# A hybrid decoder step on one NeuronCore: the head is rebuilt around untouched inputs, the end of the key search is divided around a norm, and three rotary products change engine

## The chip, the cores and the metric

The kernel runs on one core of one Trainium2 chip. The metric is the time of one execution on the device in microseconds (us), as a median of several runs. The kernel before has a median of 1154.69 us over three runs, the lowest at 1154.56 and the highest at 1155.33 us.

## The reference

One layer of a decoder for a prompt of 1024 tokens and 8 sequences of 4 new tokens each (1056 columns in all), width 1024. What matters here, cut:

```
mod = silu(c) @ w_ada + b_ada                       # one row for the prompt, 8 for the samples
shift, scale, gate = split(mod, 3)
h = rms_norm(x, g_norm) * (1 + scale) + shift
qa,ka,va,za, qi,ki,wi, qr,kr,vr,zr, ga,gr = split(h @ w_in)
# indexer: for every query the 256 best keys, by sum over 4 heads of w * relu(qi . ki)
idx = top_k(where(key <= query, index_scores(qi, wi, ki), -inf), 256)
y_a = sparse_attend(qa, ka[idx], va[idx]) * silu(za)
# retention: 8 heads (4 pairs), chunks of 128 tokens with a running state per head
q_r, k_r = rotary(qr), rotary(kr) / 8
y_r = group_norm(retention(q_r, k_r, vr)) * g_ret * silu(zr)
x = x + gate * ((sigmoid(ga) * (y_a @ w_pa) + sigmoid(gr) * (y_r @ w_pr)) @ w_out)
return rms_norm(x) * g_final, and the new keys, values, indexer keys and states
```

A prompt query below position 256 has at most 256 admissible keys, so that nothing has to be searched for it.

## The kernel before

All values that are projected stand transposed, features on partitions and the 1056 tokens in columns. Each product of full precision is made of three matmuls: weights and inputs are split into a high part (a cast to the fp32r type) and a low part (the difference), and high x high, high x low and low x high are added up (`terms`, L210 to L212). The inputs' parts are the tiles `hh` and `hl`, one of each per 128 features, k = 0 to 7; a projection of 128 output features takes 8 x 3 matmuls for each of three chunks of 352 columns.

The program's parts that matter here, in their order:

- **The head.** SyncE's queue loads a table of constants (792 columns, the first 128 of them the identity), nine tiles of x (the samples' first), and the adaLN weights `w_ada` in 16 blocks of 512 KB. ScalarE squares each tile with a sum over its row (L286), VectorE makes the reciprocal roots (`rsqrt`), VectorE or GpSimd scales the tile by them (L293), TensorE transposes it (L296) and ScalarE and VectorE copy the two halves into `xr` (L298). For each k, `h_tile` multiplies two adaLN blocks by the conditioning (`ada_rows`, L204), selects the rows of the nine conditions (L309), applies scale and shift (L313, L316), and makes `hh` (ScalarE, L317) and `hl` (VectorE or GpSimd, L318). Behind each k, `start_two` has 18 matmuls of the first two projections (indexer keys, and indexer queries of heads 0 and 1), into six accumulators.
- **The weights of the later projections.** Each 512 KB block is loaded one projection ahead (`prefetch`, L190) and split (cast L196 on ScalarE; difference L197, by turns on VectorE and GpSimd).
- **The indexer.** The rest of its queries (`project(O_QI + 128, ...)`), the scores of blocks of 128 queries against the keys (L660, L661; blocks 2 to 7 only), and those of the samples.
- **The search.** For every query the 256th largest score is found bit by bit, 31 rounds, by counting the scores above a candidate. The counts of blocks 2 to 6 run on VectorE (L743), those of block 7 and the samples on ScalarE (L750). Then comes the end of the search: `exact` sharpens the two thresholds that ScalarE's counts have found (for the samples, then block 7), and `finish` writes a mask for each of the seven score tiles, the samples' first (j = 6), then block 7 (j = 5), then blocks 2 to 6.
- **Retention.** TensorE meanwhile works through the gates' projections and four pairs of heads, one after the other (`pair`, p = 0 to 3): keys and queries are projected and rotated (`rotated`, L459 to L461, with a copy that DMAs shift by half a head), the products of keys and values by chunk (L491) are summed up by one scan on VectorE (L493), ScalarE copies the states into `SD` (L495), and TensorE multiplies them by the queries (L514). The group norm of pair p ends with L582, kept as `normed[p]`.
- **The rest.** The attention with the found keys, the remaining projections, and the output, from about 526 us on.

What sets the order: every engine has one queue of instructions, filled at build time by a scheduler that interleaves the search with retention. `tc.issue_after(x)` puts the instructions made under it behind x in the scheduler's order, where they go to the same engine's queue. In the kernel before the whole end of the search stands under

```
with tc.issue_after(normed[2].ins):
    exact(1)
    exact(0)
    for j in range(NP - 1, -1, -1):
        finish(j)
```

so that VectorE meets it only behind the third pair's norm.

## Time and profile before

| profiled execution | |
|---|---|
| its own time | 1154.27 us |
| span of the trace | 1152.5 us |
| mean granted clock of TensorE | 0.989 |
| TensorE busy (weight loads beside it) | 1090.3 us, 95% (993.7) |
| VectorE busy | 674.0 us, 58% |
| ScalarE busy | 465.1 us, 40% |
| GpSimd busy | 335.0 us, 29% |
| moved by DMA | 182.56 MB, 158 GB/s in the mean |

TensorE's share says only how often it had something to do. Where it had not, a stretch of the span has to be looked at by itself, and which engine was busy in its place. The granted clock is the part of full speed at which the chip let TensorE run. In the rows, PE is TensorE's matmuls, PEld its weight loads, DVE VectorE, ACT ScalarE, POOL GpSimd, and SPq SyncE's queue of DMAs.

### The profile page before, as it was taken

How to read it: one execution, taken by the hardware profiler on the slowest of the kernel's cores; microseconds unless marked ns; L12 is line 12 of the kernel's file. 1: busy time of each engine (PE TensorE's matmuls, PEld its weight loads, DVE VectorE, ACT ScalarE, POOL GpSimd, SP SyncE). 2: the span in 40 equal slices, each digit the busy share in tenths (PEclk: the TensorE clock that was granted, in tenths of full speed). 3: DMA queues.
4: the chain of work that ended last, by engine and by line, in shares of the span. 5: the costliest groups of instructions: out<-in, count | busy, mean ns of one | idle time of the engine just before them, and what ended most of it. 6: DMA issues, size and time to landing. Idle time of an engine off the chain costs nothing. (4 is left out here: it accounts for less than half of the span.)

```text
span 1152.5 us, 20285 instructions
## 1 busy us (share of the span) xinstructions
PE 1090.3 (95%) x8016; PEld 993.7 (86%) x8016; DVE 674.0 (58%) x1585; ACT 465.1 (40%) x894; POOL 335.0 (29%) x259
## 2 busy tenths in 40 slices
PE   4999999999999999969999999999999999989997
PEld 3889989899989999968998999877988888888886
DVE  6856449999999536993132222201246777477745
ACT  5465445655655341123243332211336656333211
POOL 3413015023311611351331212143124434375000
PEclk9999999999999999988999999999999999999999
DMA  9913235134334424412686866597899931495321
GB/s 304 264 34 111 75 104 146 53 111 140 104 90 120 141 54 139 125 37 79 221 267 199 249 193 193 178 306 262 267 269 240 236 102 66 143 275 176 114 92 55
DMA packets 157956, 182.56 MB, mean 158 GB/s; under 512 B 18901, under 2 KB 129053, under 8 KB 156774
## 3 DMA queue, kind: packets, MB, share of 16 engines
q1 hardware_dynamic: 147928, 145.56, 42.9%
q0 software_dynamic: 9856, 35.66, 9.5%
q8 instruction: 63, 1.03, 0.4%
q14 instruction: 31, 0.25, 0.1%
q10 hardware_dynamic: 78, 0.06, 0.0%
HBM read 138.86 MB, written 38.60 MB: 154 GB/s over the span
## 5 line engine op out<-in xcount | busy, mean ns | idle before, releaser
L210 PE MATMUL pj<-hh,wh 128*128 128x352 f32 x1176 | 385.4, 328 | 6.0 <-ACT qrT L446 3.2
L211 PE MATMUL pj<-hl,wh 128*128 128x352 f32 x1176 | 381.2, 324 | 0.0
L212 PE MATMUL pj<-hh,wl 128*128 128x352 f32 x1176 | 381.0, 324 | 0.0
L210 PEld LDWEIGHTS pj<-hh,wh 128*128 128x128 f32 x1176 | 221.3, 188 | 13.2 <-issue 4.4
L211 PEld LDWEIGHTS pj<-hl,wh 128*128 128x128 f32 x1176 | 221.9, 189 | 5.7 <-issue 4.9
L212 PEld LDWEIGHTS pj<-hh,wl 128*128 128x128 f32 x1176 | 221.6, 188 | 3.9 <-issue 3.4
L743 DVE TENSOR_SCALAR_CACHE_REDUCE eq<-sc,cand 128x896 bf16<-128x896 f32 (+4 forms) x155 | 135.7, 875 | 2.3
L197 POOL TENSOR_TENSOR wl<-ws,wh 128x1024 fp32r<-128x1024 f32 (+1 forms) x33 | 63.1, 1913 | 174.8 <-ACT wh L196 156.4
L196 ACT CAST wh<-ws 128x1024 fp32r<-128x1024 f32 (+1 forms) x65 | 61.1, 940 | 108.5 <-PE pj L211 64.4
L197 DVE TENSOR_TENSOR wl<-ws,wh 128x1024 fp32r<-128x1024 f32 x32 | 41.4, 1294 | 62.2 <-ACT wh L196 61.3
L1084 POOL TENSOR_SCALAR lg<-lg,st 128x1024 f32<-128x1024 f32 (+7 forms) x64 | 47.4, 746 | 76.2 <-DVE st L1083 70.9
L750 ACT ACTIVATE ra<-sc,cand 128x1024 bf16<-128x1024 f32 x31 | 35.6, 1149 | 61.6 <-DVE cand L821 61.6
L930 POOL DMA_INDIRECT kv<-in_cache_k,idx x32 | 30.9, 966 | 98.8 <-PE str L960 80.8
L1082 ACT ACTIVATE lg<-lg,st 128x1024 f32<-128x1024 f32 (+7 forms) x64 | 49.5, 775 | 22.1 <-DVE st L1081 21.8
L962 DVE COPY kt<-str 128x512 f32<-128x512 f32 x32 | 22.1, 689 | 61.3 <-PE str L960 57.6
L589 ACT ACTIVATE raw<-pj 128x352 f32<-128x352 f32 x48 | 22.1, 461 | 74.7 <-PE pj L212 67.2
L930 POOL DMA_INDIRECT kv<-in_cache_v,idx x32 | 31.1, 973 | 71.2 <-PE sx L988 42.0
L1260 PE MATMUL pj<-wol,MH 128*128 128x512 f32 (+1 forms) x136 | 51.2, 377 | 0.0
L1259 PE MATMUL pj<-woh,MH 128*128 128x512 f32 (+1 forms) x136 | 51.2, 377 | 0.0
L1261 PE MATMUL pj<-woh,ML 128*128 128x512 f32 (+1 forms) x136 | 51.2, 377 | 0.0
L1097 PE MATMUL tr<-C,lg 128*128 128x128 f32 x288 | 43.7, 275 | 1.2 <-ACT pT L1099 0.5
L962 ACT COPY kt<-str 128x512 f32<-128x512 f32 x32 | 18.8, 589 | 55.1 <-PE str L960 44.1
(341 smaller groups left out, 2073.9 us busy)
## 6 DMA issues: line engine op xcount, KB each, us to landing
ws<-in_w_in SPq DMA_DIRECT2D x51, 512.0 KB
TG<-raw SPq DMA_DIRECT2D x16, 528.0 KB
rot<-in_rot SPq DMA_DIRECT2D x8, 1056.0 KB
wa<-in_w_ada SPq DMA_DIRECT2D x16, 512.0 KB
u<-TG SPq DMA_DIRECT2D x8, 528.0 KB
RT<-u SPq DMA_DIRECT2D x8, 528.0 KB
t<-TG SPq DMA_DIRECT2D x8, 528.0 KB
u<-RT SPq DMA_DIRECT2D x8, 528.0 KB
```

The costliest lines, as they stand in the source:

```text
L196: nc.scalar.copy(wh[:, :, :n], ws[:, :, :n])
L197: (nc.vector if len(order) % 3 else nc.gpsimd).tensor_sub(wl[:, :, :n], ws[:, :, :n], f32(wh[:, :, :n]))
L210: nc.tensor.matmul(p, wh[:, k], HH[k][:, sl], start=(k == 0), stop=False)
L211: nc.tensor.matmul(p, wh[:, k], HL[k][:, sl], start=False, stop=False)
L212: nc.tensor.matmul(p, wl[:, k], HH[k][:, sl], start=False, stop=(k == KT - 1))
L743: nc.vector.tensor_scalar(junk[:n, :W], sc, thr[:n, j:j + 1], 0.0, op0=op, op1=OP.add, accum_out=cnt[:n, j:j + 1])
L930: nc.gpsimd.indirect_dma_start(out=t.rearrange("p s c -> p (s c)"), out_offset=None, in_=cache.rearrange("g (r s) h d -> (g r) (s h d)", s ...
L1082: nc.scalar.activation(l, l, AF.Exp, bias=st[:, 2:3], scale=0.125, accum_out=st[:, 3:4])
L1084: nc.gpsimd.tensor_scalar(l, l, st[:, 0:1], 0.5, op0=OP.mult, op1=OP.mult)
L1259: nc.tensor.matmul(x, MH[:, k, tk], wh[:, k], start=(k == 0), stop=False)
L1260: nc.tensor.matmul(x, MH[:, k, tk], wl[:, k], start=False, stop=False)
L1261: nc.tensor.matmul(x, ML[:, k, tk], wh[:, k], start=False, stop=(k == KT - 1))
```

## The change

The x tiles are transposed as they land. Their squares are made beside that (those of tiles 1 and 4 on VectorE, by `SQD`), and the reciprocal norms are brought into a row that is the same on all partitions, `RB`, by matmuls of a matrix of ones with diagonal matrices (`norms`). `h_tile` multiplies the transposed tile by scale and norm in one instruction, ScalarE adds the shift while it makes `hh`, and VectorE the same while it makes `hl`, both in halves of 528 columns. GpSimd has no part in it. All adaLN blocks use the x tiles' buffers, eleven in all, and they are issued in one row; the weights of later projections are issued behind the last of them, and their split stands behind the last `hh` and `hl`. The constants are loaded in two parts. Queries of the indexer are projected for columns from 256 on only, in two chunks of 400 (`late`), in the first projections and in the second. Behind the search, `exact(1)`, `exact(0)` and the samples' mask are no longer ordered behind `normed[2]`, the other six masks are. The rotation of the third pair's queries and of the fourth pair's keys and queries is on VectorE.

The core of the diff:

```diff
-SQD = ()
+SQD = (1, 4)
...
+    late = [slice(256, 656), slice(656, TT)]
+
+    def start_two(W):
+        x, y = pl(), pl()
+        parts_ = [(p[:, :sl.stop - sl.start], sl, i) for p, sl, i in
+                  zip((pj(), pj(), x[:, :512], x[:, 512:], y[:, :512]), chunks + late, (0, 0, 0, 1, 1))]
         for k in range(KT):
-            for i, p in enumerate(banks):
-                terms(p, W[i // 3], k, chunks[i % 3])
-        return banks
+            for term in range(3):
+                for p, sl, i in parts_:
+                    nc.tensor.matmul(p, W[i][term == 2][:, k], (HL if term == 1 else HH)[k][:, sl],
+                                     start=(k == 0 and term == 0), stop=(k == KT - 1 and term == 2))
...
+        def x_block(i):
+            t = SEQ[i]
+            n, x = size(t), X[t]
+            p = pl().rearrange("p (k t) -> p k t", k=KT)
+            for k in range(KT):
+                nc.tensor.transpose(p[:, k, :n], x[:n, 128 * k:128 * k + 128], ident[:n, :n])
+            sq = BI[7]
+            if t in SQD:
+                nc.vector.tensor_tensor_reduce(out=sq[:n], in0=x[:n], in1=x[:n], scale=1.0, scalar=0.0,
+                                               op0=OP.mult, op1=OP.add, accum_out=ssq[:n, i:i + 1])
+            else:
+                nc.scalar.activation(sq[:n], x[:n], AF.Square, accum_out=ssq[:n, i:i + 1])
+            for g, copy in ((slice(0, 4), nc.scalar.copy), (slice(4, 8), nc.vector.tensor_copy)):
+                copy(XT[:, g, t * 128:t * 128 + n], p[:, g, :n])
+
+        def norms(i0, i1):
...
+            r = rsqrt(sp, v, i1 - i0)
+            p, c0 = pj(), 128 * SEQ[i1 - 4]
+            for i in range(i1 - 4, i1):
+                dg = sp.tile([128, 128], F32, name="dg", bufs=3)
+                nc.vector.tensor_scalar(dg, ident, r[:, i - i0:i - i0 + 1], None, op0=OP.mult)
+                o = 128 * (i - i1 + 4)
+                nc.tensor.matmul(p[:, o:o + 128], one, dg, start=True, stop=True)
+            nc.scalar.copy(RB[:, c0:c0 + 512], p)
...
+        def h_tile(k, pm):
+            shift = BB[:, k, 0:1]
+            nc.scalar.activation(AA[:, k], pm[:, 16:25], AF.Identity, bias=cg[:, k:k + 1], scale=cols[:, 24 + k:25 + k])
+            nc.scalar.activation(shift, pm[:, 0:1], AF.Identity, bias=cols[:, k:k + 1])
+            h = XT[:, k]
+            nc.vector.scalar_tensor_tensor(h[:, :T], h[:, :T], AA[:, k, 0:1], RB[:, :T], op0=OP.mult, op1=OP.mult)
...
+            for sl in (slice(0, 528), slice(528, TT)):
+                high = nc.scalar.activation(HH[k][:, sl], h[:, sl], AF.Identity, bias=shift)
+                rest = nc.vector.scalar_tensor_tensor(HL[k][:, sl], h[:, sl], shift, f32(HH[k][:, sl]), op0=OP.add, op1=OP.subtract)
+            return high, rest
...
+        for i in range(9):
+            x_block(i)
+            if i == 4:
+                norms(0, 5)
+        norms(5, 9)
...
     def prefetch():
         if order:
             f0 = order.pop(0)
-            split.append((f0, wsplit(wp, wload(wp, w_in, f0, 128), 128)))
+            with tc.issue_after(loads[-1].ins), tc.issue_after(head_ends[0].ins), tc.issue_after(head_ends[1].ins):
+                split.append((f0, wsplit(wp, wload(wp, w_in, f0, 128), 128)))
...
-            nc.gpsimd.tensor_tensor(x, x, RT_[:, :TT], op=OP.mult)
-            nc.gpsimd.tensor_tensor(y, y, RT_[:, TT:], op=OP.mult)
-            nc.gpsimd.tensor_tensor(x, x, y, op=OP.add)
+            e = nc.vector if p + a > 2 else nc.gpsimd
+            e.tensor_tensor(x, x, RT_[:, :TT], op=OP.mult)
+            e.tensor_tensor(y, y, RT_[:, TT:], op=OP.mult)
+            e.tensor_tensor(x, x, y, op=OP.add)
...
-            project(O_QI + 128, use_qi(2))
+            project(O_QI + 128, use_qi(2), late)
...
+            exact(1)
+            exact(0)
+            finish(NP - 1)
 
             with tc.issue_after(normed[2].ins):
-                exact(1)
-                exact(0)
-                for j in range(NP - 1, -1, -1):
+                for j in range(NP - 2, -1, -1):
                     finish(j)
```

The built order shows three places. First SyncE's queue in the head, from the first adaLN block on: `wa` before and `x` from `in_w_ada` now are the adaLN blocks, `ws` the weights of projections, `ptab` a page table. Before:

```order
L324 DMA wa<-in_w_ada 128x8x128 x3
L190 DMA ws<-in_w_in 128x8x128 x2
L324 DMA wa<-in_w_ada 128x8x128 x6
L190 DMA ws<-in_w_in 128x8x128
L324 DMA wa<-in_w_ada 128x8x128 x2
L190 DMA ws<-in_w_in 128x8x128
L324 DMA wa<-in_w_ada 128x8x128 x3
L190 DMA ws<-in_w_in 128x8x128
L324 DMA wa<-in_w_ada 128x8x128
L190 DMA ws<-in_w_in 128x8x128
L324 DMA wa<-in_w_ada 128x8x128
L673 DMA ptab<-in_page_table 16x8x1 x8
```

The same place of SyncE's queue now:

```order
L348 DMA x<-in_w_ada 128x8x128 x2
L189 DMA ws<-in_w_in 128x8x128 x2
L348 DMA x<-in_w_ada 128x8x128 x14
L189 DMA ws<-in_w_in 128x8x128 x2
L703 DMA ptab<-in_page_table 16x8x1 x8
```

Of the six blocks of projection weights, two still stand early (those of the first two projections); the four others stood between adaLN blocks, and now none does.

TensorE's queue at the end of the head, from the last adaLN products on (`pt<-x,scT`); `hh_82` and `hl_90` are the parts of tile 5, `hh_83` that of tile 6, and a `pj` or `pl` stands for an accumulator:

```order
L203 MATMUL pt<-x,scT 32x128 x16
L225 MATMUL pj<-hh_82,w 128x352 x2
L225 MATMUL pl<-hh_82,w 128x352
L225 MATMUL pl<-hh_82,w 128x400 x2
L225 MATMUL pj<-hl_90,w 128x352 x2
L225 MATMUL pl<-hl_90,w 128x352
L225 MATMUL pl<-hl_90,w 128x400 x2
L225 MATMUL pj<-hh_82,w 128x352 x2
L225 MATMUL pl<-hh_82,w 128x352
L225 MATMUL pl<-hh_82,w 128x400 x2
L321 MATMUL pt<-C,ar 128x16 x2
L225 MATMUL pj<-hh_83,w 128x352 x2
```

Behind the last adaLN products stand all 15 matmuls of tile 5, three of them 128x352 and two 128x400 for each of the three terms, then the selection for tile 7, then tile 6.

VectorE's queue at the end of the search. Before, from the last count (`eq,cnt`) on; `base` holds the thresholds, `wl` a low part of weights, `zsT` and `S` belong to the third pair:

```order
L743 TENSOR_SCALAR eq,cnt<-sc_772,cand 128x384
L757 TENSOR_SCALAR inc<-cnt 128x5
L819 TENSOR_TENSOR base<-base,inc 128x7
L197 TENSOR_TENSOR wl<-ws,wh 128x1024
L484 SCALAR_TENSOR_TENSOR zsT<-zt,zsT 128x352 x2
L493 SCALAR_TENSOR_TENSOR S<-dm,pt 128x512
```

The same place of VectorE's queue now, from the two exact thresholds on (L802 to L815; `scs` are the samples' scores):

```order
L802 TENSOR_SCALAR low<-base 128x1 x2
L803 SCALAR_TENSOR_TENSOR low<-base,low 128x1 x2
L804 TENSOR_TENSOR base<-base,low 128x1 x2
L773 TENSOR_SCALAR eq,cnt<-scs,base 32x1056
L196 TENSOR_TENSOR wl<-ws,wh 128x1024
L808 TENSOR_SCALAR eq<-scs,base 32x1056
L811 TENSOR_SCALAR flag<-cnt 128x1
L809 ISA ra,low<-eq,scs 32x1056
L809 ISA low 32x1
L491 TENSOR_TENSOR qrT<-qrT,rot 128x1056
L492 TENSOR_TENSOR tmp<-tmp,rot 128x1056
L812 TENSOR_TENSOR low<-low,flag 128x1
```

and a little further on in it, to the third pair's scan (`S<-dm,pt`):

```order
L516 SCALAR_TENSOR_TENSOR zsT<-zt,zsT 128x352
L826 SCALAR_TENSOR_TENSOR ra<-eq 32x1056
L827 SCALAR_TENSOR_TENSOR ra<-ra,rem,eq 32x1056
L828 SCALAR_TENSOR_TENSOR ra<-scs,base,ra 32x1056
L516 SCALAR_TENSOR_TENSOR zsT<-zt,zsT 128x352
L829 TENSOR_SCALAR bis<-ra 32x1056
L525 SCALAR_TENSOR_TENSOR S<-dm,pt 128x512
```

Between the search's last round and the third pair's scan VectorE now has the exact thresholds, the rotation of that pair's queries (L491 to L493) and the samples' mask (L825 to L829), where it had one split and two small products. From the end of the fourth pair on all five engines' queues are what they were.

## Rows read from the trace of the kernel before

**Rows 1.** The span cut into stretches, with the busy time of each engine in us and its instructions (x), TensorE's granted clock (PEclk), the mean busy share of the DMA engines and what they moved in GB/s.

```profile
0.00:14.00 14.00, 0.07 (x1) 0.07 (x2) 3.79 (x19) 8.39 (x14) 0.20 (x4) 1.00 0.87 309
14.00:37.20 23.20, 18.20 (x222) 14.90 (x222) 22.29 (x56) 11.35 (x23) 14.19 (x9) 1.00 1.10 286
37.20:69.10 31.90, 30.88 (x293) 28.71 (x294) 19.26 (x34) 12.15 (x18) 10.20 (x4) 1.00 0.69 175
...
155.00:388.00 233.00, 223.81 (x1577) 214.61 (x1576) 213.12 (x549) 133.42 (x234) 67.19 (x33) 1.00 0.39 115
388.00:447.40 59.40, 59.40 (x467) 56.67 (x467) 20.04 (x33) 18.24 (x33) 17.59 (x9) 0.99 0.36 103
447.40:509.60 62.20, 62.16 (x436) 61.22 (x435) 61.57 (x81) 14.21 (x27) 28.44 (x11) 1.00 0.36 104
509.60:520.90 11.30, 0.00 (x0) 0.00 (x0) 11.20 (x16) 3.04 (x4) 0.00 (x0) 0.62 0.17 47
520.90:526.00 5.10, 5.09 (x32) 4.86 (x34) 0.35 (x1) 0.00 (x0) 0.00 (x0) 0.50 0.05 10
...
sum 1152.50, PE 1090.33 PEld 993.72 DVE 674.00 ACT 465.13 POOL 335.01; mean PE 99.12 PEld 90.34 DVE 61.27 ACT 42.28 POOL 30.46
```

The columns of engines are PE, PEld, DVE, ACT and POOL, in this order.

**Rows 2.** TensorE's waits by line and by what released them: us in total, how many, the longest.

```profile
PE pl L514 <- ACT SD L495: 12.6, 2, 11.4
```

**Rows 3.** The timeline of SyncE's queue in the head: start, duration, and the DMAs that it issued.

```profile
32.70 1.63 SPq L190 DMA_DIRECT2D ws<-in_w_in  x1
...
48.54 1.63 SPq L190 DMA_DIRECT2D ws<-in_w_in  x1
```

**Rows 4.** TensorE's timeline: start, duration, line, and in brackets the idle time ahead with what ended it.

```profile
26.21 1.09 PE L296 MATMUL pl<-C,x 128*128 128x128 f32 x8
...
56.21 0.51 PE L309 MATMUL pt<-C,ar 128*128 128x16 f32 x4
...
58.16 0.65 PE L204 MATMUL pt<-wa,scT 128*32 128x128 f32 x16 [0.86 <-DMA wa<-in_w_ada]
...
59.80 0.32 PE L210 MATMUL pj<-hh,x 128*128 128x352 f32 x1
...
62.20 0.32 PE L210 MATMUL pl<-hh,x 128*128 128x352 f32 x1
...
90.33 0.40 PE L661 MATMUL pl<-kil,qs 128*128 128x512 f32 x1
...
91.72 0.39 PE L661 MATMUL pl<-kil,qs 128*128 128x512 f32 x1
```

**Rows 5.** What single instructions cost: the groups on the tiles x, xr and hl in the head (ns least, median and most, with first and last start), and one row each of VectorE's and GpSimd's timelines.

```profile
L286 ACT ACTIVATE sq<-x x9: 1038/1055/1062, 5.2 to 17.4; 128x1024 bf16<-128x1024 f32 x8, 32x1024 bf16<-32x1024 f32 x1
...
L298 ACT COPY xr<-pl x9: 265/585/587, 17.3 to 33.1; 128x512 f32<-128x512 f32 x8, 128x128 f32<-128x128 f32 x1
L298 DVE COPY xr<-pl x9: 282/679/692, 18.5 to 34.5; 128x512 f32<-128x512 f32 x8, 128x128 f32<-128x128 f32 x1
...
L318 DVE TENSOR_TENSOR hl<-xr,hh x5: 1248/1257/2357, 37.7 to 65.4; 128x1056 fp32r<-128x1056 f32 x5
...
122.28 0.88 DVE L667 SCALAR_TENSOR_TENSOR sc<-rl,wsc,sc 128x640 f32<-128x640 f32 x1 [1.24 <-ACT rl L663]
...
40.79 2.87 POOL L197 TENSOR_TENSOR wl<-ws,wh 128x1024 fp32r<-128x1024 f32 x1 [6.50 <-ACT wh L196]
```

**Rows 6.** VectorE's timeline from the search's last instruction to the fourth pair's scan.

```profile
387.56 0.17 DVE L819 TENSOR_TENSOR base<-base,inc 128x7 int32<-128x7 int32 x1
...
410.02 1.22 DVE L493 TENSOR_TENSOR_SCAN S<-dm,pt 128x512 f32<-128x512 f32 x1 [4.97 <-PE pt L491]
...
447.28 0.25 DVE L582 SCALAR_TENSOR_TENSOR tmp<-pt,gT,zsT 128x32 f32<-128x32 f32 x1 [1.57 <-PE pt L579]
...
465.58 0.69 DVE L799 TENSOR_SCALAR bis<-ra 32x1056 bf16<-32x1056 f32 x1
...
475.53 2.65 DVE L797 SCALAR_TENSOR_TENSOR ra<-ra,rem,eq 128x384 f32<-128x384 f32 x1
478.22 2.72 DVE L798 SCALAR_TENSOR_TENSOR ra<-sc,base,ra 128x384 f32<-128x384 f32 x1
...
481.53 1.95 DVE L799 TENSOR_SCALAR bi<-ra 128x384 bf16<-128x384 f32 x1
...
491.13 2.91 DVE L797 SCALAR_TENSOR_TENSOR ra<-ra,rem,eq 128x640 f32<-128x640 f32 x1
494.07 2.97 DVE L798 SCALAR_TENSOR_TENSOR ra<-sc,base,ra 128x640 f32<-128x640 f32 x1
...
517.35 1.22 DVE L493 TENSOR_TENSOR_SCAN S<-dm,pt 128x512 f32<-128x512 f32 x1
```

**Rows 7.** GpSimd's timeline in the same stretch: the first instruction of each of three rotations (the third pair's queries, the fourth pair's keys and queries).

```profile
390.94 2.48 POOL L459 TENSOR_TENSOR qrT<-qrT,rot 128x1056 f32<-128x1056 f32 x1 [9.48 <-DMA tmp<-qrT]
...
474.60 3.16 POOL L459 TENSOR_TENSOR krT<-krT,rot 128x1056 f32<-128x1056 f32 x1 [15.77 <-DMA tmp<-krT]
...
489.61 3.75 POOL L459 TENSOR_TENSOR qrT<-qrT,rot 128x1056 f32<-128x1056 f32 x1 [6.35 <-DMA tmp<-qrT]
```

**Rows 8.** The fourth pair's products of keys and values on TensorE's timeline, and the copies of its states on ScalarE's.

```profile
503.68 1.15 PE L491 MATMUL pt<-vtok,kd 128*64 128x64 f32 x32
...
518.60 2.26 ACT L495 COPY SD<-S 64x512 f32<-64x512 f32 x2 [3.85 <-DVE S L493]
```

More of the change, by code (lines that the diff above doesn't have):

```diff
@@ L183, in _hybrid_step @@
     gT = cst.tile([128, 4], F32, name="gT")
+    BI = {b: selp.tile([128, (b + 1) * 128], BF, name=f"bi{b}") for b in range(8)}
+    BIS = selp.tile([NS, LK], BF, name="bis")
     def wcols(src, k, f0, n):
@@ L315, in h_tile @@
[L315 to L324 removed]
+            return pm
@@ L590, in gates @@
             nc.sync.dma_start(TG[128 * j:128 * j + 128], t)
-    BI = {b: selp.tile([128, (b + 1) * 128], BF, name=f"bi{b}") for b in range(8)}
-    BIS = selp.tile([NS, LK], BF, name="bis")
     k_out, v_out, ki_out, st_out, ks_out, vs_out, kis_out, sts_out = outs[2:]
```

138 lines of the change are left out of this document (58 added, 80 removed).

## Prediction

> **What bounds the kernel now.** I read the stretches first [rows 1]: the span cut at the places where TensorE's state changes, with every engine's busy time. The reader is to see that TensorE is the engine with work nearly everywhere, 1090.3 of 1152.5 us, and where it is not: 14 us at the start, 5.0 of the next 23.2 us, 9.2 us in all of the search (155 to 388 us), and one hole of 11.3 us at 509.6 us in which VectorE is busy throughout. Next come TensorE's waits [rows 2]: the hole is one wait of 11.4 us for the copies of the fourth pair's states (SD, line 495). Then the head (everything up to the first projections' end at 69.1 us) in the SyncE queue's issues and in TensorE's timeline [rows 3, 4]: the last adaLN weights land when product L204 starts at 58.16 us, after a wait for the DMA. Then what single instructions cost [rows 5], and VectorE, GpSimd and the fourth pair's products around the hole [rows 6 to 8].
>
> Two facts decide. The head is a stream of loads: 286 to 309 GB/s from the start [rows 1]. And the hole is VectorE's: from 447.4 to 509.6 us it is busy for 61.6 of 62.2 us and in the hole for 11.2 of 11.3, while in the 59.4 us before that it had only 20.0 us of work [rows 1]. It may not start the end of the search before the third pair's norm (L582, 447.28 us), although the search itself ended at 387.7 us [rows 6].
>
> **Fewer columns for the indexer's queries.** Only queries from 256 on are searched, so columns 0 to 255 of both query projections go. Fifteen starts of the 352-column product lie 2.40 us apart, 0.160 us each; six of the 512-column product 1.39 us, 0.232 us each [rows 4]. In between, 400 columns are 0.160 + 48 x 0.072/160 = 0.182 us, an estimate. First projections: 144 x 0.160 = 23.0 us before; 72 x 0.160 + 48 x 0.182 = 20.3 us now. Second query projection: 72 x 0.160 = 11.5 before, 48 x 0.182 = 8.7 now, in a place where TensorE is the bound (30.9 of the 31.9 us up to it busy [rows 1]): **2.8 us**. The first 2.8 us are part of the next term.
>
> **The head.** Four weight tiles for later projections stood in the queue between the adaLN weights (the first issued at 32.70 us, the fourth at 48.54 [rows 3]); now they stand behind all of them. Each is 512 KB, at 286 GB/s 1.83 us, together 7.3 us. The last adaLN weights then land near 58.2 - 7.3 = 50.9 us. Behind them TensorE has, in the built order, their 16 products, tile 5's 15 matmuls, two selections, and 30 more matmuls of tiles 6 and 7: 0.65 + 2.53 + 0.5 + 5.07 = 8.8 us (2.53 = 9 x 0.160 + 6 x 0.182; the first and the third are rows of [rows 4]). That is 59.7 us. VectorE gives a second bound. The transposes no longer wait for the norm, since they take x as it lands and the norm comes in as a row broadcast over all partitions, but every normalised tile now needs all the norms. ScalarE's squares and copies (1.06 and 0.59 us [rows 5]) end near 20 us, and the second group's norm with the weights' splits I put at 30 us. Then 8 tiles at 1.28 + 0.5 + 2 x 0.75 us (a 1024-column product, three small ones and two 528-column differences, scaled from 0.88 us for 640 columns [rows 5]) are 26 us, and the last matmuls 2: 58 to 59 us. I take **60 us against 69.1: 9.1 us less**. Bounds: 55 us, if the loads run at the 309 GB/s of the first 14 us and the norms cost nothing; 66 us, if VectorE and TensorE wait for each other at every tile.
>
> What is late next: at the seam the next projection's weights now come last, and are split only when tile 7 is done: a cast of about 1.06 us like the squares and, on GpSimd, 2.87 us for the low part [rows 5], of which TensorE's rest of tile 7 and the transposes hide about 2.4: **1.5 us** given back, with 0 and 3 as ends.
>
> **The end of the search.** The two exact thresholds and the sample's mask (lines 824 to 827, the mask for j = 6) need no norm any more. In the trace they run from 447.45 to 466.2 us [rows 6], less 1.3 us that belongs to block 7: 17 us which move into VectorE's free time, 20.0 busy of 59.4 us. Three rotations come onto VectorE, each three two-operand instructions of 1056 columns, 1.25 us by the nearest row [rows 5]: 3.8 us for the third pair's queries, 7.5 for the last pair. In exchange GpSimd is quiet there: while it rotated, from 474.60 and from 489.61 us [rows 7], VectorE's steps were stretched: 2.65 and 2.72 us for 384 columns, 2.91 and 2.97 for 640, where 640 cost 0.88 alone and 384 some 0.6, and 1.95 us for a mask's write worth about 0.4 [rows 5, 6]: 9.9 us over five instructions. So the fourth pair's scan (L493, now at 517.35 us) could come at 517.4 - 17 + 7.5 - 9.9 = 498 us, and its input is there at 504.8 us [rows 8]. The end of the search is then no longer what TensorE waits for. From the scan's start to the end of the states' copies are 3.5 us [rows 6, 8], which gives 508.4 us, and TensorE has work until 509.6: the whole hole goes, **11.35 us**. What is gone with it: TensorE came out of the hole at half the granted clock, 0.50 from 520.9 to 526.0 us [rows 1], so **2.55 us** more.
>
> The new waits are in VectorE's order. At the third pair 23.8 us of its work (the exact thresholds, one rotation, the mask, two splits) now stand ahead of that pair's scan, and the room is 387.7 to 410.0 us, 22.3 us [rows 6]; the rotation also waits in order for its DMA, which came at 390.9 us [rows 7]. In the built order the search ends one round earlier against the second pair's norm than before (three rounds behind it, where there were four), some 6 us, which covers it. I take **1 us** given back, 0 to 5 as ends. Other waits of TensorE in the search, 9.2 us, I leave as they are, with 4 us either way. From 526 us on all five engines have the same instructions in the same order.
>
> **Sum**, against the profiled execution (1154.27 us, span 1152.5): -9.1 + 1.5 - 2.8 - 11.35 - 2.55 + 1 = -23.3, so 1131.0 us. The runs' median is 0.4 us above that execution.
>
> [...] In the head TensorE's granted clock is 1.00 from the first stretch on, when it did nothing but transposes [rows 1]. [...]
>
> **Rivals.**
> 1. The end of the search stays late: a rotation that waits for its DMA holds up everything behind it on VectorE, and 6 us come back as a wait for the third or fourth pair's states. For it: VectorE is in order and the room at the third pair is short. Against it: 7 us of room at the fourth. 1137 us.
> 2. The head ends at 66 us, because tiles 0 to 7 go through VectorE one after the other, or because the norms come later than 30 us. For it: VectorE has some 41 us of work up to there (the 26, nine copies of 0.68, two splits of 1.25, two squares of about 1.2 and 22 small steps of 0.17). Against it: GpSimd, which stretches VectorE's steps in [rows 6], has no work in the new head. 1137 us.
> 3. Slower: TensorE runs the head at half the granted clock. Place: from the first transposes to the last of the first projections. Price: a tile's eight transposes take 2.2 instead of 1.09 us [rows 4], against 1.7 us in which the next tile lands (512 KB at 309 GB/s), so the first matmul comes some 3 us later, at 30 + 3.3 + 3 = 36.3 us; 20.3 us of matmuls and 8 x 0.65 us of products become 51.0, and the head ends near 87.3, 18.2 us later than now. The other terms being -14.2, that is +4.0: 1158.3 us. It decides from a head that ends after 83.3 us. Against it: the clock of 1.00 in [rows 1]; for it: behind the hole the clock stayed at 0.50 for 5.1 us of full work [rows 1].
> 4. The division does not do what it says, the queue holding the exact thresholds behind the norm anyway. The built order rules it out.
>
> **Chances.** Forecast 0.69 (1123 to 1138), rivals 1 and 2 0.12 and 0.13, rival 3 0.04, and 0.02 that the search's other waits go as well, 1122 us. The range is 1120 to 1142: below, head at 55 us and 4 us less waiting; above, rivals 1 and 2 together. A measurement of this kernel tells 0.2%, 2.3 us, from no change. Rival 3 alone reaches there: slower 0.03, same 0.01, faster 0.96.
>
> **What would show it.** Right: the first projections' last matmul between 58 and 62 us; the last adaLN weights near 51 us; no wait over 2 us for the fourth pair's states (line 514 before, 546 after); granted clock 1.00 there; the exact thresholds ahead of the third pair's scan; VectorE's mask steps near their widths' cost. Wrong: a granted clock of 0.50 before 60 us, a wait of TensorE of more than 3 us at the third pair's states, or VectorE idle before a rotation for a DMA.

## The result and the profile after

The changed kernel takes 1146.76 us, the median of six runs (1143.82 to 1152.08); the kernel before, beside it, 1154.68 (six runs, 1152.11 to 1155.45). The ratio is 0.9933, with an interval of 0.9913 to 0.9953: faster, as forecast, but by 7.9 us instead of 23, and outside the range of 1120 to 1142.

The profiled execution took 1145.85 us (span 1144.1), 8.4 less than the one before. Where TensorE stands against the kernel before can be read at instructions that both have. These are four of them in the profile before: the copy of the first pair's keys on ScalarE, the last step of the second pair's norm and of the fourth pair's on VectorE, and one stretched step of the search.

```profile
162.27 0.43 ACT L446 COPY krT<-pj 128x352 f32<-128x352 f32 x1
...
178.22 2.37 DVE L819 TENSOR_TENSOR base<-base,inc 128x7 int32<-128x7 int32 x1
...
358.64 0.25 DVE L582 SCALAR_TENSOR_TENSOR tmp<-pt,gT,zsT 128x32 f32<-128x32 f32 x1
...
556.15 0.25 DVE L582 SCALAR_TENSOR_TENSOR tmp<-pt,gT,zsT 128x32 f32<-128x32 f32 x1 [2.70 <-PE pt L579]
```

The same places in the timeline of the changed kernel, with the end of its head (L672, the first transposes of the indexer's keys) and the third pair's scan (L525) and the fourth pair's products with its states (L546):

```profile
65.55 0.38 PE L672 MATMUL pt<-C,kiT 128*128 128x128 f32 x2
...
159.46 0.44 ACT L477 COPY krT<-pj 128x352 f32<-128x352 f32 x1
...
368.21 0.24 DVE L614 SCALAR_TENSOR_TENSOR tmp<-pt,gT,zsT 128x32 f32<-128x32 f32 x1
...
415.59 1.22 DVE L525 TENSOR_TENSOR_SCAN S<-dm,pt 128x512 f32<-128x512 f32 x1 [0.72 <-PE pt L523]
...
515.20 1.05 PE L546 MATMUL pl<-qrT,SD 128*128 128x128 f32 x8
...
548.12 0.25 DVE L614 SCALAR_TENSOR_TENSOR tmp<-pt,gT,zsT 128x32 f32<-128x32 f32 x1 [2.72 <-PE pt L611]
```

| place | before, us | after, us | difference |
|---|---|---|---|
| end of the head | 69.1 | 65.55 | -3.5 |
| first pair's keys | 162.27 | 159.46 | -2.8 |
| second pair's norm | 358.64 | 368.21 | **+9.6** |
| third pair's scan | 410.02 | 415.59 | +5.6 |
| fourth pair's states used | 520.9 | 515.20 | -5.7 |
| fourth pair's norm | 556.15 | 548.12 | -8.0 |
| span | 1152.5 | 1144.1 | -8.4 |

So the hole went as forecast, the head gave little more than a third of what was forecast (3.5 of 9.1 us), and between the first pair and the second pair's norm the changed kernel lost 12.4 us. The stretches show all three (columns as in [rows 1]). First those of the head, cut where the granted clock changes:

```profile
14.00:23.00 9.00, 6.74 (x77) 5.80 (x77) 7.93 (x37) 6.42 (x13) 0.00 (x0) 1.00 1.16 305
23.00:29.80 6.80, 5.17 (x44) 3.72 (x44) 3.12 (x10) 1.83 (x4) 0.00 (x0) 0.50 1.16 288
29.80:33.20 3.40, 2.20 (x38) 1.39 (x37) 2.67 (x4) 2.34 (x6) 0.00 (x0) 0.99 1.16 292
33.20:40.00 6.80, 6.73 (x49) 6.21 (x50) 6.18 (x12) 3.79 (x9) 0.00 (x0) 0.50 1.16 291
40.00:65.50 25.50, 25.30 (x256) 23.86 (x255) 16.74 (x32) 13.35 (x28) 1.46 (x1) 1.00 0.50 127
```

The granted clock does not show how the head begins. It reads 1.00 from the start on, but up to 9.4 us the transposes of 128x128 follow each other at 0.213 us, and from there on at 0.109 us. Up to then TensorE had done nothing but transposes. These are ten of them ahead of 9.4 us and eight behind it, on TensorE's timeline:

```profile
7.01 2.39 PE L283 MATMUL pl<-C,x 128*128 128x128 f32 x10
...
11.50 1.09 PE L283 MATMUL pl<-C,x 128*128 128x128 f32 x8
```

Then the search, the third pair, the end of the search, and the place of the former hole:

```profile
155.00:388.00 233.00, 219.28 (x1531) 210.50 (x1532) 217.31 (x545) 131.85 (x229) 62.97 (x31) 0.99 0.35 101
...
388.00:447.40 59.40, 59.40 (x469) 56.66 (x468) 38.68 (x67) 18.79 (x34) 12.81 (x7) 1.00 0.44 127
447.40:509.60 62.20, 62.20 (x398) 61.17 (x396) 47.60 (x66) 15.13 (x28) 7.91 (x5) 1.00 0.35 104
509.60:520.90 11.30, 11.30 (x140) 10.78 (x140) 5.31 (x7) 5.16 (x9) 0.00 (x0) 1.00 0.20 51
520.90:526.00 5.10, 5.10 (x59) 3.71 (x57) 1.01 (x2) 1.33 (x3) 0.00 (x0) 1.00 0.00 0
```

From 388 to 526 us TensorE is busy throughout, at a granted clock of 1.00, and VectorE has room (47.6 of 62.2 us, where it had 61.6). In the search TensorE idles for 13.7 us (233.0 - 219.28), against 9.2 before, and VectorE is busy for 217.3 of 233 us, where it was 213.1. The search's first round ended 6.8 us earlier than before (165.9 against 172.7 us), its last at the same time (387.8 against 387.6). What became longer is seen in VectorE's groups. The three short steps that end a round, before (busy us and mean ns behind the bar, then idle time) ...

```profile
L757 DVE TENSOR_SCALAR inc<-cnt 128x5 int32<-128x5 f32 x31 | 12.7, 409 | 0.8
L819 DVE TENSOR_TENSOR base<-base,inc 128x7 int32<-128x7 int32 x31 | 11.7, 378 | 0.8
L821 DVE TENSOR_SCALAR cand<-base 128x7 int32<-128x7 int32 x30 | 9.4, 313 | 0.9
```

... and after, with the largest count above them:

```profile
L773 DVE TENSOR_SCALAR_CACHE_REDUCE eq<-sc,cand 128x896 bf16<-128x896 f32 x31 | 35.5, 1145 | 0.9
...
L787 DVE TENSOR_SCALAR inc<-cnt 128x5 int32<-128x5 f32 x31 | 18.5, 598 | 0.9
L849 DVE TENSOR_TENSOR base<-base,inc 128x7 int32<-128x7 int32 x31 | 14.3, 462 | 0.8
L851 DVE TENSOR_SCALAR cand<-base 128x7 int32<-128x7 int32 x30 | 7.2, 240 | 0.8
```

Together 33.8 us before and 40.0 after, while the counts, which are most of the work, did not change (35.5 us and 1145 ns; 1146 ns before). Steps of five or seven columns take 0.17 us when they are alone. Why some take 2.4 us is seen on VectorE's and GpSimd's timelines at 186 to 192 us of the changed kernel:

```profile
186.61 2.47 DVE L787 TENSOR_SCALAR inc<-cnt 128x5 int32<-128x5 f32 x1
189.12 2.38 DVE L849 TENSOR_TENSOR base<-base,inc 128x7 int32<-128x7 int32 x1
191.53 0.17 DVE L851 TENSOR_SCALAR cand<-base 128x7 int32<-128x7 int32 x1
...
186.60 2.46 POOL L491 TENSOR_TENSOR qrT<-qrT,rot 128x1056 f32<-128x1056 f32 x1 [6.08 <-DVE eq L773]
189.01 2.46 POOL L492 TENSOR_TENSOR tmp<-tmp,rot 128x1056 f32<-128x1056 f32 x1
```

In the search, all of VectorE's instructions that took over 0.25 us more than others of their kind ran beside GpSimd: by this count over the timeline 11 of them with 19.9 us in excess before, and 16 with 26.2 us after. I call this excess the stretch. Each of the 16 ends within some 30 ns behind the GpSimd instruction that ran when it started, so that the loss is the rest of that instruction. The one-column steps of the same rounds (L789) are not touched: nine of them started beside GpSimd and took 0.14 to 0.16 us. So in this trace the short steps wait (2.47 us beside an instruction of 2.46) and the counts do not (seven counts of 896 columns that ran beside GpSimd took 1145 to 1148 ns, the mean of all 31 is 1145). What in the hardware tells them apart is not shown.

TensorE's longest waits in the search (155 to 388 us) are for copies of retention on ScalarE:

```profile
PE pj L209 <- ACT qs L429: 4.4, 2, 2.2
PE pt L462 <- ACT tmp L477: 3.6, 2, 2.3
```

Behind two of these waits, at 238.1 and 302.9 us, the granted clock was at 0.50 for 3.4 us each (half clock, as I call it from here on). My reading is that the stretch delays these copies, because VectorE and ScalarE have them in their queues between the rounds. The experiments ask whether that is so. Is it GpSimd's instructions that cost the head's gain (theory A), the order of the new queues (B), the half clock in the head (C), or the tail's own work on VectorE, which is the exact thresholds and the rotations ahead of the third pair (D)?

### The profile page after: what moved, and what is told of

Read it like the earlier page. It is cut to its first block, busy times and chain, and to the rows that moved or that the text cites. A ratio compares the mean times of both kernels' runs of the same rounds, so it can differ in the third digit from the quotient of the medians.

```text
span 1144.1 us, 20239 instructions
## 1 busy us (share of the span) xinstructions
PE 1095.3 (96%) x7986; PEld 994.7 (87%) x7986; DVE 675.3 (59%) x1594; ACT 469.7 (41%) x910; POOL 283.4 (25%) x238
## 5 line engine op out<-in xcount | busy, mean ns | idle before, releaser
L209 PE MATMUL pj<-hh,wh 128*128 128x352 f32 (+1 forms) x1168 | 384.6, 329 | 11.1 <-ACT qs L429 4.4
L211 PE MATMUL pj<-hh,wl 128*128 128x352 f32 (+1 forms) x1168 | 379.4, 325 | 0.0
L210 PE MATMUL pj<-hl,wh 128*128 128x352 f32 (+1 forms) x1168 | 378.7, 324 | 0.0
```

Source lines behind the costliest of these rows:

```text
L209: nc.tensor.matmul(p, wh[:, k], HH[k][:, sl], start=(k == 0), stop=False)
L210: nc.tensor.matmul(p, wh[:, k], HL[k][:, sl], start=False, stop=False)
L211: nc.tensor.matmul(p, wl[:, k], HH[k][:, sl], start=False, stop=(k == KT - 1))
```

## Experiments

Times are medians of five or more executions, one experiment apart, and each ratio is against the kernel before on the same chip. That kernel took 1154.5 to 1157.3 us on the three chips of the experiments, so that the ratios are the safer comparison where two versions ran on different chips.

### The end of the search alone

The kernel before with these edits:

```diff
-            nc.gpsimd.tensor_tensor(x, x, RT_[:, :TT], op=OP.mult)
+            e = nc.vector if p + a > 2 else nc.gpsimd
+            e.tensor_tensor(x, x, RT_[:, :TT], op=OP.mult)
...
+            exact(1)
+            exact(0)
+            finish(NP - 1)
             with tc.issue_after(normed[2].ins):
-                exact(1)
-                exact(0)
-                for j in range(NP - 1, -1, -1):
+                for j in range(NP - 2, -1, -1):
```

> The kernel before with the divided end of the search and the three rotations on VectorE alone; head and query columns as before. The order of all five queues up to the end of the search is that of the kernel before. Theory A (between the head and the third pair VectorE's search sets the pace, its short steps wait for GpSimd's instructions, and this ate what the new head gave): the whole gain of the hole and of the clock behind it is here, 13.9 us, so 1140 us, and 1137 if the two stretched steps near 377 us (3.9 us) go with the rotation that leaves GpSimd. Rival D (the loss in the search comes from the rotations on VectorE or from the exact thresholds in front of the third pair): TensorE waits more than 5 us at the third pair, 1146 us or more.

Measured: 1147.85 us, ratio 0.9926 (0.9902 to 0.9949). The hole went here too, but TensorE waits at the third pair:

```profile
418.54 2.55 PE L515 MATMUL pl<-qrT,SD 128*128 128x128 f32 x14 [4.23 <-ACT SD L496]
```

4.2 us, and half clock behind it for 3.4. With TensorE on time at the third pair, the work that VectorE now has ahead of that pair's scan is too long. The time is the one that theory D asked for, and its wait is there, if shorter than the 5 us it named; theory A's 1140 us left that out. In the search itself D fails: the rounds take 215 us as before, the second pair's norm comes at 359.5 us (358.6 before), and the stretch is 19 us. The loss in the search thus comes with the head and the query columns. In the changed kernel nothing is seen of the wait at the third pair, since TensorE is itself 5.6 us late there.

### The head and the query columns alone

The changed kernel with the opposite edits.

> The changed kernel with the end of the search behind the third pair's norm again and all rotations on GpSimd: new head and fewer query columns alone. Theory A: the search is as in the changed kernel (222 us from its first to its last round, where it was 215), the third pair's norm comes near 452 us, the hole is back with 11.4 us and the half clock behind it, and the time is 1145.9 + 13.9 = 1160 us, slower than before by 5. Rival D: the head keeps its 5 to 6 us to the end, 1148 to 1150 us.

Measured: 1159.84 us, ratio 1.0025 (1.0008 to 1.0042): slower than before. The new head with fewer query columns alone costs time, and theory A's number holds. The stretch in the search is 26.1 us by the same count, again in 16 steps, so that it is not an accident of one execution.

### GpSimd's rotations in four pieces

```diff
-            e = nc.vector if p + a > 2 else nc.gpsimd
-            e.tensor_tensor(x, x, RT_[:, :TT], op=OP.mult)
+            for e, g in ((nc.vector, [slice(0, TT)]),) if p + a > 2 else ((nc.gpsimd, [slice(264 * i, 264 * i + 264) for i in range(4)]),):
+                for s in g:
+                    e.tensor_tensor(x[:, s], x[:, s], RT_[:, s], op=OP.mult)
...
```

and the two other instructions likewise.

> The changed kernel with GpSimd's five rotations cut into four pieces of 264 columns each, the same work. Theory A: a step of VectorE then waits for a piece of some 0.65 us instead of an instruction of 2.45 us; of the 26 us by which steps are stretched in the search 15 come from rotations, and 10 of them go. The search takes some 212 us instead of 222, TensorE's idle time between 155 and 388 us falls from 13.7 to under 8 us, and the time falls by 5 to 9 us, to 1137 to 1141. Theory B (the new waits of TensorE come from where the steps of retention stand between the rounds in the new order, GpSimd does not matter): no change, 1145 to 1148 us.

Measured: 1134.95 us, ratio 0.9813 (0.9795 to 0.9831), 11.8 us below the changed kernel. The search takes 212.2 us, TensorE's idle time from 155 us to its end is 5.3 us, and the three short steps cost 28.9 us:

```profile
L790 DVE TENSOR_SCALAR inc<-cnt 128x5 int32<-128x5 f32 x31 | 10.9, 352 | 0.8
L852 DVE TENSOR_TENSOR base<-base,inc 128x7 int32<-128x7 int32 x31 | 9.8, 315 | 0.9
L854 DVE TENSOR_SCALAR cand<-base 128x7 int32<-128x7 int32 x30 | 8.2, 273 | 0.8
```

The time is below what theory A asked for. But the built order had moved as well, 46 rows of VectorE, so B was not yet out.

### The same order, with pieces

```diff
-[slice(264 * i, 264 * i + 264) for i in range(4)]
+[slice(0, 288), slice(288, 544), slice(544, 800), slice(800, 1056)]
```

> The changed kernel with GpSimd's five rotations in pieces of 288, 256, 256 and 256 columns. With these sizes TensorE, ScalarE and VectorE have the order of the changed kernel (three rows of VectorE behind the search apart), while the equal pieces of e3_cut4 had moved 46 rows of VectorE. Theory A (a step of VectorE waits for the end of the GpSimd instruction that runs): as e3_cut4, 1135 to 1139 us, the steps' stretch in the search near 18 us. Rival B (the gain of e3_cut4 came from its order): 1145 to 1148 us.

Measured: 1137.82 us, ratio 0.9853 (0.9829 to 0.9878), 8.9 us below the changed kernel in practically its own order. A rotation's four pieces, on GpSimd's timeline, take 2.90 us together, where one instruction took 2.46, and a short step that meets one takes 0.5 to 0.7 us:

```profile
185.02 2.90 POOL L492 TENSOR_TENSOR qrT<-qrT,rot 128x288 f32<-128x288 f32 x4 [5.02 <-DVE cand L854]
187.87 2.90 POOL L494 TENSOR_TENSOR tmp<-tmp,rot 128x288 f32<-128x288 f32 x4
...
189.62 0.48 DVE L790 TENSOR_SCALAR inc<-cnt 128x5 int32<-128x5 f32 x1
190.13 0.66 DVE L852 TENSOR_TENSOR base<-base,inc 128x7 int32<-128x7 int32 x1
190.83 0.73 DVE L854 TENSOR_SCALAR cand<-base 128x7 int32<-128x7 int32 x1
...
356.52 0.25 DVE L617 SCALAR_TENSOR_TENSOR tmp<-pt,gT,zsT 128x32 f32<-128x32 f32 x1
```

The stretch is 17.4 us by the same count, as expected. The second pair's norm comes at 356.5 instead of 368.2 us. Of these 11.7 us, 2.6 were there before the search, since the half clock fell at another place in this execution's head, which ended at 63.0 us; 9.1 us are won from the first pair's keys on. Theory A holds against B: with the order kept, shorter instructions on GpSimd are worth 8.9 us.

### TensorE kept at work in the head

```diff
                 ada_rows(pm[:, 128 * o:128 * o + 128], lambda c: wa[k][o][:, c])
+                for _ in range(8 if k < 3 else 0):
+                    nc.tensor.transpose(pm[:, 256:384], ident, ident)
```

> The changed kernel with 48 transposes of the identity put into TensorE's idle times between 20 and 33 us, into an unused part of an accumulator. Theory C (idle time of TensorE in the head brings the half clock at 23 and at 33 us): the granted clock stays at 1.00 there and the head ends near 62 us instead of 65.6. Theory A adds that these 3.5 us are not kept through the search: 1143 to 1147 us. If they are kept, 1142. If the clock falls all the same, the head ends at 66 to 67 us and the time is 1146 to 1148.

Measured: 1146.31 us, ratio 0.9925 (0.9907 to 0.9943). The granted clock stays at 1.00 and the head ends at 63.2 us, 2.35 earlier, in spite of 48 transposes more:

```profile
21.00:30.00 9.00, 7.96 (x108) 6.19 (x100) 5.68 (x18) 3.99 (x8) 0.00 (x0) 1.00 1.15 289
30.00:40.00 10.00, 9.69 (x115) 8.88 (x116) 8.62 (x15) 6.01 (x13) 0.00 (x0) 1.00 1.12 287
```

Theory C holds in this execution: with the idle times filled the clock stays at 1.00 up to the head's end. The median moved by 0.45 us, less than these executions can tell apart, but the loss that theory A added is not where it put it. In the profiled execution (1144.19 us, the fastest of its six) the second pair's norm and the fourth pair's come 7.9 us earlier than in the changed kernel:

```profile
360.31 0.25 DVE L616 SCALAR_TENSOR_TENSOR tmp<-pt,gT,zsT 128x32 f32<-128x32 f32 x1
...
540.23 0.25 DVE L616 SCALAR_TENSOR_TENSOR tmp<-pt,gT,zsT 128x32 f32<-128x32 f32 x1 [2.72 <-PE pt L613]
```

The lead of 2.4 us grew in the search, where 14 steps were stretched instead of 16, although VectorE's order from 26 us on is that of the changed kernel. So how many steps meet GpSimd hangs on the moment at which the search begins, too. What went was lost behind the fourth pair: from its norm to the end this execution takes 602.2 us, the changed kernel's 595.9. TensorE idles there for 2.8 us more, and half clock costs 3.4 us more. Why is not shown.

### The new head without a third of its matmuls

```diff
-            for term in range(3):
+            for term in (0, 2):
```

> The changed kernel without the product of high weights and low inputs in the first two projections: 40 of their 120 matmuls, 6.8 us, are left out. One look, at the head alone. Theory G (from its first matmul at 32.6 us on TensorE itself is the bound of the new head): the first transposes of the indexer's keys come 5 to 7 us earlier, at 59 to 61 us instead of 65.4. Theory H (what the prediction took: the loads, or VectorE's tiles one after the other, are the bound): 64 to 66 us.

A single execution, 1132.73 us. Its head ends at 58.47 instead of 65.55 us:

```profile
58.47 0.44 PE L672 MATMUL pt<-C,kiT 128*128 128x128 f32 x2 [0.60 <-ACT kiT L660]
```

That is 7.1 us earlier for 6.8 us of matmuls left out. Part of it is the clock, which was at half from 24.5 to 34.7 us here. The kernel with the same order and pieces (e5_same_order) has the changed kernel's head and half clock at the same place, from 24.4 to 34.6 us; its head ended at 63.0 us. Against that, 4.5 us are won, and TensorE now idles for 2.0 of the 26.1 us from its first matmul on. Theory H is out, and theory G holds: TensorE is the bound of the new head, though no longer the only one with a third of its matmuls gone. The total is not read, since the order behind the head moved too.

### Three rounds fewer

```diff
-            for k in range(30, -1, -1):
+            for k in range(30, 2, -1):
```

> The changed kernel with 28 rounds of the search instead of 31: the three lowest bits of the thresholds are left out. Theory A (VectorE's search sets the pace from the first round to the third pair): the search ends 21 us earlier, and TensorE takes what it has lost there, 13.7 us of idle time and 3.4 us of half clock, 1129 to 1133 us. Rival F (TensorE is the bound there and waits for VectorE only at a few places): at most 5 us, 1141 to 1146 us.

Measured: 1148.58 us, ratio 0.9931 (0.9906 to 0.9955): no gain, and theory A falls in this part. Rival F's 1141 to 1146 us were not reached either. The last round ends at 369.0 us instead of 387.8, yet the third pair's scan comes at 416.4:

```profile
368.99 0.17 DVE L849 TENSOR_TENSOR base<-base,inc 128x7 int32<-128x7 int32 x1
...
416.39 1.22 DVE L525 TENSOR_TENSOR_SCAN S<-dm,pt 128x512 f32<-128x512 f32 x1 [4.96 <-PE pt L523]
```

VectorE now idles for 5 us before it. All of TensorE's waits of over 2 us have ended by 345 us, where retention's steps stand between rounds that this kernel still has. So the search does not hold TensorE by its end. As I read it, it holds TensorE round by round, up to the second pair's norm.

### The old head with pieces

The first experiment's kernel (end of the search alone) with

```diff
-            e.tensor_tensor(x, x, RT_[:, :TT], op=OP.mult)
+                for s in g:
+                    e.tensor_tensor(x[:, s], x[:, s], RT_[:, s], op=OP.mult)
```

and the same slices `g` as above.

> The kernel before with the divided end of the search, the three rotations on VectorE and GpSimd's other five rotations in four pieces: what e3_cut4 is, with the old head and all query columns. Theory A: with the stretch gone the new head's gain is kept, so this one is slower than e3_cut4 by the 3.5 us of the head and the 1.3 to 2.6 us of the columns, 1140 to 1141 us, and up to 1147 if TensorE waits at the third pair as in e1_tail_only. Rival E (the new head is worth nothing in any case, since the search sets the end): 1135 us.

Measured: 1145.39 us, ratio 0.9905 (0.9882 to 0.9929), 10.4 us above the changed kernel with the same pieces. The new head is worth something once the stretch is shorter: the search begins 9.6 us later with the old head, and TensorE waits 3.9 us at the third pair again, which is the case for which up to 1147 us were expected. Rival E is out.

### All long GpSimd instructions in pieces

```diff
+            for q in range(0, 8, 2):
+                nc.gpsimd.tensor_sub(wl[:, q:q + 2, :n], ws[:, q:q + 2, :n], f32(wh[:, q:q + 2, :n]))
...
+        for q in range(0, 18, 6):
+            nc.gpsimd.tensor_tensor(yc[:, q:q + 6], o18[:, q:q + 6], mu[:, q:q + 6].unsqueeze(2).to_broadcast([128, 6, 64]), op=OP.add)
```

> e3_cut4 with GpSimd's splits of weights in four pieces and its two instructions per norm in three pieces as well; the order moves with it. Theory A: in e3_cut4 some 9 of 18 us of stretch still come from these long instructions; 6 of them go, and TensorE, idle for 5.3 us between 155 and 388 us and 3.4 us at half clock, takes 2 to 5 of them: 1130 to 1133 us. If TensorE's rest of idle time is not VectorE's: 1134 to 1136.

Measured: 1131.17 us, ratio 0.9778 (0.9754 to 0.9802): the fastest version, 15.6 us below the changed kernel and inside the expected range. The sum of stretch hardly fell, from 18.4 to 16.3 us (33 short meetings in place of 24), and TensorE's idle time from 155 to 376 us went from 5.3 to 4.0 us; the order moved too, so not all of the 3.8 us below the kernel with only the rotations in pieces is shown to be stretch.

### The two together, and the queries' rotation back

The last kernel, with the lines of the filler put in:

```diff
+                for _ in range(8 if k < 3 else 0):
+                    nc.tensor.transpose(pm[:, 256:384], ident, ident)
```

> e7_cut_all with the 48 transposes of e4_filler. The clock stays at 1.00 up to 60 us and the head ends 2.5 us earlier. Theory A: with the stretch mostly gone an earlier head is kept, 1128 to 1129 us. Rival E (the search sets the end whatever the head does): 1131 us.

Measured: 1133.62 us, ratio 0.9823 (0.9801 to 0.9845), no faster than without the transposes and outside both theories. The clock did not stay at 1.00 either. In the profiled execution it was at half for 3.4 us, with TensorE busy throughout:

```profile
26.60:30.00 3.40, 3.40 (x28) 2.75 (x27) 0.00 (x0) 0.00 (x0) 0.00 (x0) 0.50 1.11 281
```

The head ended at 64.8 us, 1.0 earlier than without the transposes and not 2.5. A wait of TensorE at the third pair, 1.4 us, is there, which the kernel without the transposes does not have. But at the fourth pair's norm this execution is only 1.0 us behind that kernel's; 2.8 us more come behind it, as in the first experiment with the transposes. I took the wait for the cause, VectorE's work at the third pair being too long for an earlier TensorE. To take that work away:

```diff
-            ... if p + a > 2 else ((nc.gpsimd, ...
+            ... if p > 2 else ((nc.gpsimd, ...
```

> e10_cut_all_filler with the rotation of the third pair's queries back on GpSimd, in four pieces; TensorE's and ScalarE's order is unchanged. Theory A, with VectorE's work between the search's last round and the third pair's scan as the next bound: 3.8 us of it go, TensorE's wait of 1.4 us for the third pair's states in e10_cut_all_filler goes, and the time falls by 1 to 3 us, to 1131 to 1133. Rival (the third pair is not what holds it): 1133 to 1135 us.

Measured: 1143.43 us, ratio 0.9898 (0.9875 to 0.9921), by the ratios 8.7 us slower, and outside both expectations. TensorE now waits for GpSimd, and the granted clock was at half around that wait for 6.8 us:

```profile
393.87 0.79 PE L543 MATMUL pl<-qrT,krT 64*128 64x128 f32 x2 [6.03 <-POOL qrT L502]
...
381.43 4.28 POOL L498 TENSOR_TENSOR qrT<-qrT,rot 128x264 f32<-128x264 f32 x4 [5.67 <-DMA tmp<-qrT]
385.67 7.17 POOL L500 TENSOR_TENSOR tmp<-tmp,rot 128x264 f32<-128x264 f32 x4
392.80 5.63 POOL L502 TENSOR_TENSOR qrT<-qrT,tmp 128x264 f32<-128x264 f32 x4
```

Beside VectorE's exact thresholds and the samples' mask the same pieces take 4.3 to 7.2 us instead of 2.9: it is now GpSimd's instructions that are stretched. In this kernel the rotation is better on VectorE.

### The kernel before, with pieces and nothing else

The rotations are all on GpSimd here, each in four pieces; the weight split and the norms are in pieces as in e7_cut_all:

```diff
-            nc.gpsimd.tensor_tensor(x, x, RT_[:, :TT], op=OP.mult)
+            g = [slice(264 * i, 264 * i + 264) for i in range(4)]
+            for s in g:
+                nc.gpsimd.tensor_tensor(x[:, s], x[:, s], RT_[:, s], op=OP.mult)
...
```

> The kernel before with the GpSimd instructions of e7_cut_all in pieces, all eight rotations included; nothing of the change. Theory A: TensorE's waits in the search, 7.3 us, fall by 3 to 4 us, and the end of the search, of which 9.9 us were stretch, shortens by about 8, so that the hole of 11.35 us falls to some 3: 1140 to 1143 us. Rival B (pieces help only the changed order): 1153 to 1156 us.

Measured: 1144.27 us, ratio 0.9913 (0.9898 to 0.9928), 1.3 us above the range of theory A and far from rival B. The fourth pair's scan comes at 506.5 instead of 517.35 us:

```profile
506.48 1.21 DVE L501 TENSOR_TENSOR_SCAN S<-dm,pt 128x512 f32<-128x512 f32 x1
```

TensorE waits there no more; 3.1 us of another wait, at 483.7 us, take its place, with half clock around it for 6.8 us. Pieces alone, without any of the change, give 10.2 us, more than the change did.

## Why the prediction was wrong

- **Fewer columns and the seam:** with the seam, 1.3 us less were forecast; from the head's end to the first pair's keys the kernel lost 0.7 (-3.5 to -2.8). The price of a matmul was right: in the second query projection they start 0.182 us apart in the median. The seam cost nothing, since TensorE goes from the head into that projection without a pause. But its waits up to the first pair's keys are 2.5 us, where they were 0.8, and its busy time fell by 1.0 us instead of 2.8; where the other 1.8 us went stays open.
- **The head:** the step that failed is the sum of 8.8 us of TensorE's work behind the last adaLN weights. It took for granted that TensorE waits for them. The loads ran as forecast, even better (DMA falls silent at 52 us, with two more blocks of 512 KB behind the last adaLN one), but TensorE came to the products only at 55.67 us. From its first matmul on it is the bound: idle for 0.4 of 32.9 us. Of these 32.9 us the half clock made 3.6 (29.3 with the transposes in the idle times). Half of the adaLN products were missing in my sums too: the row with 0.65 us [rows 4] is one of the two blocks of a tile, and both take 1.08. The end came at 65.55, inside the bounds of 55 to 66 and near the 66 us of rival 2, but not by its mechanism.
- **Rival 3** happened in part: the granted clock was 0.50 from 23.0 to 29.8 and from 33.2 to 40.0 us. In the first of these TensorE was partly waiting (busy for 5.17 of 6.80 us); the second nearly doubled some 3.4 us of work (its 352-column matmuls start 0.293 us apart, those behind it 0.161). The price is 2 to 4 us and not 18: 3.6 us from the first matmul on, and 2.35 us at the head's end, since the 48 transposes beside which the clock stayed at 1.00 (e4_filler) take time of their own. The case that I made against this rival was misread. The granted clock of 1.00 in [rows 1] does not stand for full speed: in the kernel before, too, the first transposes of 128x128, up to 20.5 us, start 0.213 us apart, and the next ones, from 22.7 us on, 0.109. Nor had TensorE only transposes there: up to 14 us it had next to nothing to do (0.07 us [rows 1]), and then transposes and adaLN products by turns.
- **The hole:** right. 11.35 us and the half clock behind it went; from the third pair's scan to the fourth pair's norm the difference turns from +5.6 to -8.0, 13.6 us against 13.9 forecast. In the first experiment the hole is gone with the old head; in the second it is back with the new one.
- **The third pair:** the new wait was forecast at 1 us, with 0 to 5. In the changed kernel there is none, but only because TensorE is late; with the old head it is 4.2 us and half clock. The argument that the search ends a round earlier in the order and so covers it was wrong: the search ended at 387.8 us, as before (387.6), since it took 6.9 us longer, 6.3 of them stretch.
- **The step that decided:** "Other waits of TensorE in the search, 9.2 us, I leave as they are, with 4 us either way". They did not stay. From the first pair's keys to the second pair's norm the kernel lost 12.4 us: 6.4 more of waits, 3.4 of half clock, and 2.6 in TensorE's busy time for the same matmuls, which stay open. Of the 12.4 us 4.0 came back by the third pair's scan, ahead of which the kernel before waits (1.9 us, ended at 385.5) and runs at half clock (0.50 from 386.0 to 389.4 us) and this one does not. I had seen that GpSimd stretches VectorE's steps, in [rows 6 and 7], and used it only behind the search, where it helped my sum. In the search VectorE was busy for 213.1 of 233 us [rows 1], so that little room was left for more stretch, and I took the stretch there for a constant. It grew from 19.9 to 26.2 us.

How much of the loss hangs on the length of GpSimd's instructions is read from four kernels with the divided end of the search. From the first pair's keys to the second pair's norm they take

| | GpSimd's rotations whole | in pieces |
|---|---|---|
| old head, all query columns | 196.2 us (e1_tail_only) | 195.8 us (e6_old_head_cut4) |
| new head, fewer query columns | 208.7 us (the changed kernel) | 199.7 us (e5_same_order) |

The new head costs 12.6 us there with whole instructions and 3.8 us with pieces in the same order. In the time of the whole program, by the ratios, it wins nothing with whole instructions (0.8 us lost, within the noise) and 6.0 us with pieces. So most of the loss in the search is shown to hang on the length of GpSimd's instructions, and the rest is not explained.

The sum of the profiles: -3.5 + 0.7 + 8.4 (to the third pair) - 13.6 - 0.4 = -8.4 us. Of the 14.9 us that the forecast had too much, 5.6 lie in the head, 2.0 in the columns and the seam, and 7.4 between the first pair's keys and the third pair's scan.

What stays open: why the short steps meet GpSimd more often in the changed kernel (16 times instead of 11). The order moved by one round and the search starts earlier against retention; both changed at once. The kernel with transposes in the head says that the start alone matters, with 14 meetings in the changed kernel's order. The half clocks in the search (3.4 us of loss in the changed kernel) were not taken away by themselves.

## What to carry to other kernels

An engine that is busy for nine tenths of a stretch, as VectorE is here (217.3 of 233 us), can be its second bound: a gain on the first one there has to be argued through the second's queue, and what stretches its steps belongs in the sum. Where VectorE runs chains of short steps, try GpSimd's instructions in short pieces: here cutting them cost 0.4 us an instruction (2.90 us for 2.46) and gave 8.9 us in the same order (e5_same_order), and 15.6 with the order free and the other long instructions cut as well (e7_cut_all). And before a stream of loads is called the bound, add up the engine behind it from its first instruction on, not only from the last load.

## What the runs showed of the hardware

- In the changed kernel's search, VectorE's steps on five or seven columns that started during a GpSimd instruction waited for its end: 0.17 us alone, up to 2.47 beside a 1056-column product; beside pieces of 256 to 288 columns 0.48 to 0.73 (e5_same_order). The one-column steps of the same rounds (0.14 to 0.16 us) and the counts of 896 columns with an accumulator (a mean of 1145 ns, 1146 in the kernel before) were untouched.
- It went the other way as well: four pieces on GpSimd took 2.9 us in the search and up to 7.2 beside VectorE's exact thresholds and the samples' mask (e12_queries_back).
- The granted clock read 1.00 while TensorE's first transposes of 128x128 ran at half of their later rate (0.213 against 0.109 us each, up to 9.4 us in the changed kernel). Look at the distance of like instructions, too.
- In the changed kernel the granted clock fell to half at 23.0 us, after 9 us in which TensorE was busy for 6.7. With 48 transposes of the identity in the idle times it stayed at 1.00 in two profiled executions (e4_filler, e12_queries_back) and fell for 3.4 us, at 26.6 us, in a third (e10_cut_all_filler). The length of the last pause did not tell: in the changed kernel the clock fell to half behind waits of 2.2 and 2.3 us (ended at 236.8 and 301.9 us), and did not behind one of 2.2 us (ended at 344.9 us).
